# One decoder layer on one core: the program's order taken from a simulated timeline of all engines

## The chip, the core and the metric

The kernel runs on one core of a Trainium2 chip. A core has five engines with an instruction queue each: PE (matrix multiply), DVE (vector), ACT (scalar), POOL (GpSimd) and SP (here it only issues DMAs). An engine takes its own queue strictly in order and waits for the others by semaphores. The metric is the device time of one execution in microseconds (us), as the median of several.

## What is computed

One layer of a hybrid decoder, 1024 positions by 1024 channels, float32. Cut to what matters:

```python
x1 = LN1(a * x + 0.5 * swiglu(x, ffn1))             # FF = 2816, a = 2 ** 0.25
z  = x1 @ w_in                                      # 1024 x (2048 + 1824) columns
ret = silu(g) * group_norm(retention(q, k, v))      # 8 heads of 64, chunks of 128
rw  = (group_norm(rwkv7_scan(r, w, k, v, kk, a)) + bonus) * gate   # 8 heads of 64
x2 = LN2(a * x1 + concat(ret, rw) @ w_out)
x3 = LN3(a * x2 + 0.5 * swiglu(x2, ffn2))
out = x3 + sigmoid(x3 @ ple_w_gate + b) * (p @ ple_w_proj)

def step(state, inp):                               # rwkv7_scan, one position
    r_t, w_t, k_t, v_t, kk_t, b_t = inp
    sa = einsum('bhvk,bhk->bhv', state, kk_t)
    state = state * w_t - sa * b_t + v_t * k_t     # outer products
    return state, einsum('bhvk,bhk->bhv', state, r_t)
```

Each RWKV head carries a 64 by 64 state through all positions, so its chunks of 128 positions form a chain.

## The kernel before

**Stages.** The first feed-forward layer (`ffn_up`, line 152, tiles f1m; `ffn_down`, line 415, tiles f1qa, f1qb) runs to about 683 us of the profile, LN1 and the first z tiles to 757, the mixer to 1591, the second feed-forward layer (f2m, f2qa, f2qb) to 2270, and LN3 with the gated embedding (`ple`, line 1269, tile pg) to the end. Large matmuls are done in three fp32r products of operands split in two: ACT copies the high part (line 47), DVE subtracts for the low part (line 48), PE multiplies (`mm3`, lines 61, 62, 63).

**The mixer** (`mixer`, line 1205). z is made in tiles of 128 columns by `z_tile` (line 646): two raw loads on SP (line 52, raw_win), the split (hi_win, lo_win), 48 matmuls of 128x512 into tile z, an ACT copy (zs, line 659) and a store on SP (line 660). Its pools have one buffer for the split weights and one for zs, two for the raw weights, two for z. The first tiles, zf, come from `z_first` (line 662) during LN1. The gate's sums (gps, line 782) and the LoRA parts follow.

RWKV runs as eight **units** s_h, 0_0 to 3_1: a pair of heads, and one half of the 1024 positions, four chunks of 128. For a unit there are

- `rw_inputs` (line 906): smoothing, decay (ACT tanh wthw, a DVE scan csw, POOL ccw, ACT exp ePw and eMw), normalised keys (sqw, sspw, rnpw, kkw), wkw, rkw, the bonus bnpw;
- `rw_operands` (line 986): m1pw (line 1001) masked into M1 (line 1004), which is stored to device memory (line 1006, scrw), as the operands are (lines 1010 to 1016, opsw);
- `substitution` (line 1018), for two units at once: loads iltw (line 1027), 31 pairs of DVE rows (itw, line 1035, and ixw, line 1037), a store (line 1039, scsw);
- `doublings` (line 1043): loads Xd (line 1049) and M1w, then i1w to i5w on PE with DVE between (lines 1062 to 1083);
- `rw_chunks` (line 1087): for each chunk a load opsw (line 1097, four buffers), scpw on PE, masked into scz (lines 1116, 1117), then a chain through chw: lines 1122, 1125, ACT rhsw (1127), 1130, ACT saw (1132), 1134 and 1135, the next state wst (line 1144), and the outputs 1147 to 1152; at the end a group norm (`group_norm`, line 790, tile gnyw), transposes ytpw, ACT and POOL (wow, lines 1161 to 1163), and a store into mixed (line 1164).

`retention` (line 815) runs beside it. `w_out_group` (line 1182) reads rows of mixed (line 1178), splits them, and multiplies them with w_out into tile wopo, 384 matmuls in all, which DVE adds into xacc (line 1201); the last groups need mixed of units 3_0 and 3_1.

**What sets the order.** The code is written stage by stage, and a scheduler in the framework makes the order of each queue from it: of the instructions that are ready it takes the one of highest priority, where priority falls with place in the code, and advances a model of the machine. z tiles and w_out rows of a stage are **fillers**: they get a priority lower by 300 than their place would give, so they stand where nothing else is ready. The stage loop, shortened:

```python
for s in range(-1, 8):
    ...
    W[s + 2] = inputs(s + 2); self.rw_operands(W[s + 2])
    self.doublings(W[s])
    if s % 2 and s + 2 < 8: self.substitution([W[s + 1], W[s + 2]])
    self.rw_chunks(W[s], mixed[4 + u])
    with self.tc.high_priority(offset=20): self.retention(u, h, rt(u), mixed[u])
    with self.tc.issue_after(self.gate):
        for f in fill.get(s, ()):
            with self.tc.high_priority(offset=FILLER): (rw if f[0] == "w" else rt)(int(f[1]))
        ...
            with self.tc.high_priority(offset=FILLER): self.w_out_group(ks, mixed, halves, ks == (7, 3))
```

## Time and profile before

| what | us |
|---|---|
| median of 3 runs | 2381.23 (2372.49 to 2385.13) |
| the profiled execution | 2393.63 |
| its span | 2391.8 |
| PE, weight loads on PE | 2274.9 busy (95%), 1823.5 (76%) |
| DVE | 1558.6 (65%) |
| ACT | 849.5 (36%) |
| POOL | 636.0 (27%) |

Busy time is summed over the span; a matmul's end is modelled, so records of matmuls overlap. The mean granted clock of TensorE is 0.965 of full speed over the span. The slices and stretches below say where in the span an engine works, the timeline in which order, and the waits who held whom.

### The profile page before, as it was taken

To read this page: it belongs to the slowest core of one execution; us is meant where nothing else is said; L and a number is where in the kernel's file an instruction comes from. 1 tells how busy PE (TensorE), PEld (TensorE's weight loads), DVE (VectorE), ACT (ScalarE), POOL (GpSimd) and SP (SyncE) were. 2 spreads that over 40 slices of the span, in tenths; PEclk is the share of its full clock that TensorE was granted. 3 is DMA by queue.
4 is the path that set the end of the run, shared out by engine and by line. 5 is a ranking of instruction groups with operands and counts; after the bars stand their busy time and mean duration, and the time that the engine had idled before them with its cause. 6 is when DMAs were issued, how large, how long until landed. Compare 5 with 4: busy or idle time off the path is not lost.

```text
span 2391.8 us, 30775 instructions
## 1 busy us (share of the span) xinstructions
PE 2274.9 (95%) x10753; PEld 1823.5 (76%) x10753; DVE 1558.6 (65%) x2524; ACT 849.5 (36%) x1434; POOL 636.0 (27%) x535
## 2 busy tenths in 40 slices
PE   6999999999999789899899899988999999999999
PEld 5888888788786567777777677766888788788777
DVE  7677776665872365764664645779767677866962
ACT  4323323244643323232233222254322232445550
POOL 3346454100111112221222212015555543000210
PEclk8999999999999889999999887999999999999999
DMA  4355555587245545454454445232555553975321
GB/s 142 118 163 178 170 182 167 176 323 228 81 152 163 180 134 170 155 161 137 155 155 140 151 140 172 93 110 73 161 177 167 181 160 130 342 271 158 113 75 40
DMA packets 319985, 379.53 MB, mean 159 GB/s; under 512 B 36915, under 2 KB 188054, under 8 KB 319830
## 3 DMA queue, kind: packets, MB, share of 16 engines
q1 hardware_dynamic: 302576, 358.64, 46.5%
q0 software_dynamic: 3328, 12.06, 1.3%
q10 hardware_dynamic: 13926, 6.87, 1.0%
q8 instruction: 85, 1.39, 0.2%
q14 instruction: 70, 0.57, 0.1%
HBM read 256.37 MB, written 121.11 MB: 158 GB/s over the span
## 4 chain that ended last, share of the span: by engine, by line
PE 80%; DVE 11%; DMA 3%; issue 3%; ACT 2%; POOL 1%; SPq 0%; ACTq 0%; DVEq 0%; POOLq 0%
PE f1m L61 6%; PE f1m L62 6%; PE f1m L63 6%; PE f2m L61 5%; PE f2m L63 5%; PE f2m L62 5%; PE z L63 3%; PE z L61 3%; PE z L62 3%; PE f1qa L62 1%; PE f1qa L61 1%; PE f1qa L63 1%; PE scpw L1108 1%; PE pg L62 1%; PE pg L61 1%
## 5 line engine op out<-in xcount | busy, mean ns | idle before, releaser
L61 PE MATMUL z<-x1Th,hi_win 128*128 128x512 f32 x448 | 189.1, 422 | 6.9 <-ACT hi_win L47 6.9
L63 PE MATMUL z<-x1Th,lo_win 128*128 128x512 f32 x448 | 188.8, 422 | 4.9 <-DVE lo_win L48 4.9
L62 PE MATMUL z<-x1Tl,hi_win 128*128 128x512 f32 x448 | 186.7, 417 | 0.0
L61 PEld LDWEIGHTS z<-x1Th,hi_win 128*128 128x128 f32 x448 | 86.9, 194 | 28.1 <-ACT hi_win L47 8.1
L63 PEld LDWEIGHTS z<-x1Th,lo_win 128*128 128x128 f32 x448 | 86.6, 193 | 27.8 <-DVE lo_win L48 7.4
L62 PEld LDWEIGHTS z<-x1Tl,hi_win 128*128 128x128 f32 x448 | 86.8, 194 | 18.4 <-issue 1.5
L149 POOL TENSOR_TENSOR f2tb<-f2tb,f2tb 128x512 f32<-128x512 f32 x44 | 69.8, 1586 | 85.9 <-DMA f2tb<-in_ffn_w_down 77.1
L48 DVE TENSOR_TENSOR f1hl<-f1s,f1hh 128x512 fp32r<-128x512 f32 x63 | 45.5, 723 | 61.7 <-ACT f1hh L47 61.7
L48 DVE TENSOR_TENSOR lo_win<-raw_win,hi_win 128x512 fp32r<-128x512 f32 x56 | 39.9, 718 | 66.1 <-ACT hi_win L47 58.1
L149 POOL TENSOR_TENSOR f1tb<-f1tb,f1tb 128x512 f32<-128x512 f32 x44 | 70.5, 1603 | 31.7 <-DMA f1tb<-in_ffn_w_down 23.4
L48 DVE TENSOR_TENSOR f2hl<-f2s,f2hh 128x512 fp32r<-128x512 f32 x63 | 44.8, 711 | 44.6 <-ACT f2hh L47 44.6
L47 ACT CAST f1hh<-f1s 128x512 fp32r<-128x512 f32 x63 | 39.2, 622 | 91.4 <-PE f1qa L62 38.6
L47 ACT CAST f2hh<-f2s 128x512 fp32r<-128x512 f32 x63 | 39.2, 623 | 87.8 <-PE f2qa L62 35.1
L659 ACT COPY zs<-z 128x512 f32<-128x512 f32 x56 | 32.6, 583 | 103.3 <-PE z L63 84.7
L62 PE MATMUL f2qa<-f2vl,f2hh 128*128 128x512 f32 x164 | 64.1, 391 | 0.8 <-DVE f2vl L48 0.8
L63 PE MATMUL f2qa<-f2vh,f2hl 128*128 128x512 f32 x164 | 64.0, 390 | 0.6 <-DVE f2hl L48 0.6
L1143 POOL TENSOR_SCALAR sfw<-wst,few 64x64 f32<-64x64 f32 x48 | 24.0, 500 | 150.7 <-DVE wst L1144 100.1
L179 DVE TENSOR_TENSOR f1U<-f1m,f1U 128x512 f32<-128x512 f32 x50 | 33.5, 687 | 46.8 <-PE f1m L63 46.8
L62 PE MATMUL f1qa<-f1vl,f1hh 128*128 128x512 f32 x164 | 63.9, 389 | 0.0
L63 PE MATMUL f1qa<-f1vh,f1hl 128*128 128x512 f32 x164 | 63.8, 389 | 0.0
L61 PE MATMUL f1qa<-f1vh,f1hh 128*128 128x512 f32 x164 | 63.3, 389 | 0.0
L108 DVE TENSOR_TENSOR f2S<-f2w 128x512 f32<-128x512 f32 x22 | 17.7, 810 | 68.8 <-DMA f2w<-in_ffn_w_gu 64.2
(783 smaller groups left out, 7151.9 us busy)
## 6 DMA issues: line engine op xcount, KB each, us to landing
f1w<-in_ffn_w_gu SPq DMA_DIRECT2D x44, 512.0 KB
f2w<-in_ffn_w_gu SPq DMA_DIRECT2D x44, 512.0 KB
f1s<-hd SPq DMA_DIRECT2D x63, 256.0 KB
f2s<-hd SPq DMA_DIRECT2D x63, 256.0 KB
zs<-zs SPq DMA_DIRECT2D x56, 256.0 KB
opsw<-opsw SPq DMA_DIRECT2D x32, 448.0 KB
raw_win<-in_w_in SPq DMA_DIRECT2D x54, 256.0 KB
f1tb<-in_ffn_w_down SPq DMA_DIRECT2D x44, 256.0 KB
```

The source lines that it names most:

```text
L47: self.last_split = self.nc.scalar.copy(hi, src).ins
L48: (eng or self.nc.vector).tensor_tensor(out=lo, in0=src, in1=hi, op=ALU.subtract)
L61: mm(ps, a[0], b[0], start=first, stop=False)
L62: mm(ps, a[0], b[1], start=False, stop=False)
L63: mm(ps, a[1], b[0], start=False, stop=last)
L108: sub = lambda o, a, b, op=ALU.subtract: V.tensor_tensor(out=o, in0=a, in1=b, op=op)
L149: nc.gpsimd.tensor_tensor(out=t, in0=a, in1=b, op=ALU.subtract)
L179: add = lambda out, a, b, eng=V: eng.tensor_tensor(out=out, in0=a, in1=b, op=ALU.add)
L659: nc.scalar.copy(zs, ps)
L1108: nc.tensor.matmul(ps[e][:, 0:2 * P], kp[rr], ar[rr].rearrange("p a t -> p (a t)"), start=True, stop=True)
L1143: nc.gpsimd.tensor_scalar(out=sf[rr], in0=st[rr, rr], scalar1=fe[rr, c:c + 1], scalar2=None, op0=ALU.mult)
```

## The change

One argument of the context in which the program is built. With it, the scheduler advances another machine model when it picks the next ready instruction: a simulated timeline of all engines, in place of its default model. No instruction's operands change; on ACT there are two more loads of a function table (34, before 32), and the scheduler's semaphore instructions differ by some.

```diff
-    with tile.TileContext(nc) as tc:
+    with tile.TileContext(nc, schedule_with_timeline_sim=True) as tc:
         hybrid_layer(tc, A)
```

What this does to the queues is seen at three places. First, PE in the chunks of unit 0_0, chunk 3 before and chunk 2 after (chw is the chunk's chain, z the filler). Before:

```order
3609 L63 MATMUL z_0_7201<-x1Th,lo_win_1_7198 128x512
3610 L61 MATMUL z_0_7201<-x1Th,hi_win_1_7197 128x512
3611 L1130 MATMUL chw_03_7638<-rhsw_03_7642,XTw_0_7463 128x64 x2
3612 L62 MATMUL z_0_7201<-x1Tl_3704,hi_win_1_7197 128x512
3613 L63 MATMUL z_0_7201<-x1Th,lo_win_1_7198 128x512
3614 L61 MATMUL z_0_7201<-x1Th,hi_win_1_7197 128x512
3615 L1134 MATMUL chw_03_7638<-opsw_03_7626 128x128
3616 L1135 MATMUL chw_03_7638<-saw_03_7646,opsw_03_7626 128x128
3617 L62 MATMUL z_0_7201<-x1Tl_3705,hi_win_1_7197 128x512
3618 L63 MATMUL z_0_7201<-x1Th,lo_win_1_7198 128x512
```

After:

```order
3802 L61 MATMUL z_1_7975<-x1Th,hi_win_0_7937 128x512
3803 L62 MATMUL z_1_7975<-x1Tl_3700,hi_win_0_7937 128x512
3804 L1134 MATMUL chw_02_7602<-opsw_02_7590 128x128
3805 L1135 MATMUL chw_02_7602<-saw_02_7610,opsw_02_7590 128x128
3806 L63 MATMUL z_0_7947<-x1Th,lo_win_1_7944 128x512
3807 L61 MATMUL z_0_7947<-x1Th,hi_win_1_7943 128x512
3808 L62 MATMUL z_0_7947<-x1Tl_3703,hi_win_1_7943 128x512
3809 L63 MATMUL z_0_7947<-x1Th,lo_win_1_7944 128x512
3810 L61 MATMUL z_0_7947<-x1Th,hi_win_1_7943 128x512
3811 L62 MATMUL z_0_7947<-x1Tl_3704,hi_win_1_7943 128x512
```

Before, two to four z stand between two steps of the chain; after, the run that begins at 3806 has 22 z to the next chw, at 3828, and the one that ends at 3803 is as dense.

Second, DVE at the substitution for units 1_0 and 1_1 (itw and ixw are its rows, M the matrix M1, scz the chunk's masked scores, wst its state, gnyw the group norm of unit 0_1). Before:

```order
930 L802 TENSOR_REDUCE gstw_1_8444<-gsqw_1_8449 128x8
931 L804 RECIPROCAL gstw_1_8444<-gstw_1_8444 128x8
932 L805 TENSOR_TENSOR gnyw_1_8445<-gnyw_1_8445,gstw_1_8444 128x512
933 L1035 TENSOR_TENSOR itw_00_8210<-iltw_0_8198,ixw_0_8207 64x31
934 L1037 TENSOR_TENSOR ixw_0_8207<-ixw_0_8207,itw_00_8210 64x31
935 L1035 TENSOR_TENSOR itw_01_8213<-iltw_0_8198,ixw_0_8207 64x60
936 L1037 TENSOR_TENSOR ixw_0_8207<-ixw_0_8207,itw_01_8213 64x30x2
937 L1035 TENSOR_TENSOR itw_02_8216<-iltw_0_8198,ixw_0_8207 64x87
```

After:

```order
909 L1004 COPY_PREDICATED M_6343<-mask,m1pw_10_8089 128x512
910 L1004 COPY_PREDICATED M_6343<-mask,m1pw_11_8090 128x512
911 L1144 SCALAR_TENSOR_TENSOR wst_6360<-chw_10_8320,few_1_6794,sfw_100_8332 64x64
912 L1144 SCALAR_TENSOR_TENSOR wst_6360<-chw_10_8320,few_1_6794,sfw_101_8335 64x64
913 L754 SCALAR_TENSOR_TENSOR wvw_0_8870<-wzvw_0_8867,pcol,smvw_0_8871 128x512
914 L1116 COPY_PREDICATED scz_6347<-mask,scpw_120_8382 128x256
915 L1035 TENSOR_TENSOR itw_00_8210<-iltw_0_8198,ixw_0_8207 64x31
916 L1037 TENSOR_TENSOR ixw_0_8207<-ixw_0_8207,itw_00_8210 64x31
917 L1117 COPY_PREDICATED scz_6347<-mask,scpw_120_8382 128x128
918 L1116 COPY_PREDICATED scz_6349<-mask,scpw_121_8383 128x256
```

Before, the substitution begins behind unit 0_1's group norm, 22 rows behind M1 (910); after, five rows behind M1, among the masks of unit 0_1's third chunk, and the group norm stands behind it, at 1004 to 1010.

Third, PE at the end of the last unit (ytpw and ytpr are the transposes of the last RWKV and retention outputs, wopo the w_out matmuls). Before:

```order
5323 L812 MATMUL ytpw_1_12573<-ident,gnyw_1_12563 128x128 x4
5324 L855 MATMUL rspr_11_12633<-zqr_1_12595,zkr_1_12605 128x128
5325 L855 MATMUL rspr_10_12632<-zqr_1_12595,zkr_1_12605 128x128
5326 L855 MATMUL rspr_11_12633<-zqr_1_12595,zkr_1_12605 128x128
5327 L855 MATMUL rspr_10_12632<-zqr_1_12595,zkr_1_12605 128x128
5328 L855 MATMUL rspr_11_12633<-zqr_1_12595,zkr_1_12605 128x128
5329 L61 MATMUL wopo_1_0_0_11795<-mw 128x512
5330 L62 MATMUL wopo_1_0_0_11795<-mw 128x512
```

After:

```order
5539 L1152 MATMUL chw_13_12546<-saw_13_12554,scz_6351 128x64
5540 L1151 MATMUL chw_13_12546<-opsw_13_12534,scz_6353 128x64
5541 L1152 MATMUL chw_13_12546<-saw_13_12554,scz_6353 128x64
5542 L812 MATMUL ytpw_1_12573<-ident,gnyw_1_12563 128x128 x4
5543 L812 MATMUL ytpr_1_12685<-ident,gnyr_1_12670 128x128 x4
5544 L61 MATMUL wopo_1_0_0_12982<-mw 128x512
5545 L62 MATMUL wopo_1_0_0_12982<-mw 128x512
5546 L61 MATMUL wopo_1_1_0_12990<-mw 128x512
```

Before, 336 of the 384 wopo matmuls stand behind ytpw; after, 48 do, from 5544 to 5591, and the others stand among units 2_1, 3_0 and 3_1.

## Rows read from the trace of the kernel before

**Rows 1.** The page's slices: tenths of each fortieth of the span (59.8 us) that PE was busy.

```profile
PE   6999999999999789899899899988999999999999
```

**Rows 2.** Stretches, PE. Columns: stretch, length, PE busy (matmul records), granted clock, DMA share, GB/s.

```profile
100.00:460.00 360.00, 360.00 (x1590) 1.00 0.50 163
...
757.00:872.00 115.00, 92.83 (x354) 0.87 0.54 172
872.00:922.00 50.00, 49.23 (x313) 0.93 0.49 152
922.00:1038.00 116.00, 108.70 (x592) 0.96 0.48 150
...
1398.00:1447.00 49.00, 47.30 (x276) 0.79 0.51 152
1447.00:1502.00 55.00, 54.98 (x285) 0.75 0.43 140
...
872.00:1502.00 630.00, 597.72 (x3381) 0.92 0.48 149
...
1057.00:1085.00 28.00, 27.89 (x177) 1.00 0.49 144
```

**Rows 3.** The same view for the z tiles' matmuls alone.

```profile
872.00:1502.00 630.00, 287.20 (x975) 0.92 0.48 149
...
1057.00:1085.00 28.00, 11.81 (x41) 1.00 0.49 144
```

**Rows 4.** The same view for the w_out matmuls (wopo) alone, behind the last unit.

```profile
1502.00:1592.00 90.00, 83.35 (x337) 1.00 0.32 106
```

**Rows 5.** PE in order of time: start, duration, engine, line, tiles; z matmuls, first i1.

```profile
1014.48 0.39 PE L61 MATMUL z<-x1Th,hi_win 128*128 128x512 f32 x1
...
1018.68 0.39 PE L61 MATMUL z<-x1Th,hi_win 128*128 128x512 f32 x1
...
1037.97 1.95 PE L1062 MATMUL i1w<-Xd,M1w 128*128 128x128 f32 x16
```

**Rows 6.** Stretches, PE's weight loads: stretch, length, PEld busy (records), granted clock.

```profile
100.00:460.00 360.00, 298.01 (x1589) 1.00 0.50 163
872.00:1502.00 630.00, 466.55 (x3380) 0.92 0.48 149
```

**Rows 7.** In order of time, all engines, behind the last unit: transposes to store.

```profile
1502.31 0.60 PE L812 MATMUL ytpw<-ident,gnyw 128*128 128x128 f32 x4
...
1507.63 0.32 SPq L1164 DMA_DIRECT2D mixed<-wow  x1
```

**Rows 8.** The same for the inputs of unit 2_0, first and last step.

```profile
1036.81 0.67 ACT L935 ACTIVATE wthw<-wpw,pder 128x512 f32<-128x512 f32 x1
...
1055.97 1.49 PE L1001 MATMUL m1pw<-arw,bbw 64*128 64x128 f32 x16
```

**Rows 9.** The same for two steps of a chunk of unit 0_1.

```profile
983.51 0.27 ACT L1127 COPY rhsw<-chw 128x128 f32<-128x128 f32 x1 [0.46 <-PE chw L1125]
...
983.83 0.66 PE L1130 MATMUL chw<-rhsw,XTw 128*128 128x64 f32 x4
```

**Rows 10.** The same on PE at LN1's second half: two of four groups.

```profile
686.98 0.60 PE L80 MATMUL tp<-ident,f1acc 128*128 128x128 f32 x4
...
689.75 0.60 PE L80 MATMUL tp<-ident,f1acc 128*128 128x128 f32 x4
```

**Rows 11.** The same, the substitution run in unit 0_1: M1's store, first row, its store.

```profile
968.77 0.34 SPq L1006 DMA_DIRECT2D scrw<-M  x1
...
990.78 0.18 DVE L1035 TENSOR_TENSOR itw<-iltw,ixw 64x31 f32<-64x31 f32 x1
...
1029.21 0.47 SPq L1039 DMA_DIRECT2D scsw<-ixw  x1
```

**Rows 12.** Waits, 757 to 1591: who waited for whom, us, times, longest.

```profile
SPq L660 <- ACT zs L659: 139.7, 33, 13.0
...
DVE wst L1144 <- PE chw L1135: 36.7, 15, 6.1
```

## The prediction

> **What bounds the kernel now.** I read the 40 slices first [rows 1]. PE's digit is 9 at both sides of the middle of the span; slices 12 to 27, the mixer, are the only long stretch with lower ones. The change is one line, but it gives every engine's queue a new order. Comparing the two orders, PE's is the same or nearly so in both feed-forward layers; rows move by hundreds of places only in the mixer, by some tens where LN1, the second feed-forward layer and the last stage begin. So the question is what the mixer, 757 to 1591 us, gives up.
>
> The mixer is eight RWKV units in a chain. I take a unit from its first i1 matmul to the next unit's: 50, 116, 47, 132, 53, 128, 49, 55 us 630 in all (the stretches of the first two, the last two and all eight stand in [rows 2]). The even ones are short; the odd ones are long, because the substitution for the next two units runs in them on DVE, and PE has little left but z matmuls. Then come 89 us of w_out matmuls, from 1502 to 1591 [rows 4, 7].
>
> How idle is PE in those 630 us? The busy column says 597.7 of 630 [rows 2], so 32 idle. I don't believe that as the amount to gain: a z matmul is listed as 0.39 us, but 18 of them start within 4.20, 0.23 apart [rows 5], so the ends overlap, and before a wait the modelled end covers a part of it. I therefore count by starts. A z or a w_out matmul, of one shape, costs 0.23. The small fp32 matmuls are two records each; 16 records of i1 take 1.95 [rows 5], 16 of m1p 1.49 [rows 8], and 136 of them share 28 us of unit 1_0 with 41 z, which leaves them 18.6 or 0.136 each, short waits included [rows 2, 3]. I take 0.12, ends 0.10 and 0.136. In the units stand 3381 records, 975 of z, 48 of w_out, so 2358 small ones [rows 2, 3]: 224 + 11 + 283 = 518 us of work, and 112 of idle (ends 74 and 159).
>
> The Trainium skill ("Perfetto Trace Analysis", Identifying the Most-Contended Engine) says that matmul busy time is no good measure because matmuls are pipelined, and to go by the share of weight loads. That share is 83% where PE never waits (298 of 360, from 100 to 460) and 74% in the units (467 of 630) [rows 2, 6]: by that, 11% or about 67 us idle. If the three kinds of idle below shrink in the same proportion, 72 becomes 43, the small work 328, and the units end 16 us later: 2344. The trace agrees that the busy column misleads; on the amount the two readings differ.
>
> **The change part by part.** Work is the same on all engines but two table loads more on ACT. What moves:
>
> 1. *The fillers.* Counted in the two orders between the first i1 of each unit, z (with the first tiles' zf): ahead of unit 0_0 514 before and 566 after; in the units 974 and 922. The w_out matmuls: in the units 48 before and 336 after; behind the last recurrence row 336 and 48. So 288 of 384 w_out matmuls leave the tail, 288 x 0.23 = 66 us, and go between the steps of units 2_1, 3_0 and 3_1, from which 52 z make room.
>
> 2. *The tail.* Now 1502 to 1591 holds 337 w_out matmuls [rows 4], 78 us of work and 11 of everything else. After: 48 matmuls, 11 us. But the last rows of mixed come only behind the last group norm, and that chain loses its cover: from the last ytp at 1502.3 by ACT, two POOL rows and other POOL work between to the store at 1507.6 [rows 7], 4 without that; a store, the load behind it and the first use take 8.8 elsewhere (1029.2 to 1038.0) [rows 5, 11]. So with the split 14 us are exposed. LN2 and the first transposes, which now lie beside w_out matmuls, may be late by 5. 11 + 14 + 5 = 30 instead of 89: **-59** (ends -72 with the chain covered by the last retention rows, -45 if chain and LN2 take 14 more).
>
> 3. *The units.* Filler work after: (922 + 336) x 0.23 = 289, before 235; small work unchanged, 283. Idle after, in three pieces. (a) In six units the new order has a part with almost no fillers: doublings, the next unit's inputs and the first chunk, some 75 small matmuls, before the fillers start. The inputs chain is tanh to m1p, 1036.8 to 1057.5 in unit 1_0, step by step through ACT, DVE and POOL [rows 8], so this part is about 22 us with 138 records x 0.12 = 16.6 of work: 5.4 idle x 6 = 32. (b) In the filled part each gap between chunk steps holds 13 to 23 z, 3 to 5 us, where the trace shows 0.5 to be needed: rhs on ACT 983.51 to 983.78 behind one chw, the next chw at 983.83 [rows 9]. There PE should be the bound. I take 5%, the share that is idle even by the busy column (32 of 630) [rows 2], of 390 us: 20. (c) Units 3_0 and 3_1 now have 104 us, 76 fillers and 485 small records [rows 2], so 29 idle; 74 more fillers take about 9 of it: 20. Sum 72 us idle, and units of 289 + 283 + 72 = 644: **+14**. No waits in (b) and half of (a): -22; 10% in (b): +34.
>
> 4. *Ahead of unit 0_0.* 52 more z is +12 us of work. 757 to 872 has 92.8 us busy of 115 even by the busy column [rows 2], so there is room; the new order puts 118 more z in the first wait behind the gate sums and 52 more between the second m1p and i1, where 130 stand now. I take -15. Against that, at LN1's second half four groups of transposes come 2.75 us apart, filled with 10 zf each [rows 10]; after, most zf run earlier and 12 are left: +7. Together **-8** (ends -20, +10).
>
> 5. *The substitution.* Before, it starts behind the group norm: M1 is stored at 968.8, and the loads follow, but the first DVE row comes at 990.8 and the store behind the last at 1029.2, then Xd and i1 at 1038 [rows 5, 11]. After, its rows start some five DVE rows behind M1 and lie among the chunk's masks and states. The chain of an odd unit is then inputs 22, M1 to loads 8, its own rows with others between as now 38, to i1 9: 77 us. The unit's PE work, about 85, is longer, so it is hidden and costs nothing more. It is what lets the odd units fall from 116 to 132 to some 80 to 90; the even ones grow to as much.
>
> 6. *Start of both feed-forward layers, LN3 and the last stage.* Places move by up to 76 there, and the tables on ACT are two loads more. PE in the start of the second layer has its own waits; I take 0, ends -8 and +8.
>
> Sum: -59 + 14 - 8 = **-53**. On the profiled execution, 2393.6, that gives 2341; the median of the runs is 12 lower, so 2381.2 - 53 = **2328 us**.
>
> **Rivals.** *A, the fillers cover more:* no waits in the filled parts, a better clock: units -22, front -20, tail -65: -107, 2274. For it: the granted clock is 0.75 and 0.79 in the last two units, which have fewest fillers, and 0.96 from 922 to 1038 with many z [rows 2]; a unit with more fillers may be granted more. Against: the parts with no fillers remain.
>
> *B, the new order idles as large a share as the old:* 112 of 630, 17.8%. Then the units take 572 / 0.822 = 696, +66, and nothing is left of the tail: 2381 - 59 + 66 - 8 = 2380. For it: the 72 are a count on an order, and the order fixes who is ahead of whom on SP too. SP stood 13.0 us behind one z store, 139.7 in 33 such waits [rows 12], with the loads of operands and weights queued behind. In the new order each z store still waits for its filler, and PE reaches fillers later relative to the chunk.
>
> *C, slower: the substitution in DVE's queue.* Its 62 rows now stand among masks and states that wait for PE; states alone wait 36.7 us, 15 times, for chunk matmuls [rows 12], and these now stand behind 3 to 5 us of fillers. If 14 more such waits of 4 us fall between the first and the last row, the chain grows from 77 to 133 and the unit from 85 to 133, and with three substitutions that is +144: 2472. It decides from 26 us a substitution on: 8 until the chain is longer than PE's work, then 53 / 3 = 18; at 33 the time is 2402. Against it: in unit 0_1 the order has few such rows ahead of the first half of the substitution.
>
> *D, nothing changes:* excluded by the order, unless the moves cancel.
>
> **How the numbers follow.** Forecast, 2290 to 2362: 0.48. A, 2250 to 2290: 0.17. B, 2362 to 2393: 0.2. C: 0.15, mostly 2393 to 2450. The range leaves out a fifth, the lowest part of A and most of C: 2262 to 2400. A measurement of this kernel tells about 0.5%, 12 us, from no change. Faster than 2369: 0.48 + 0.17 + 0.09 = 0.74; within: 0.11; slower: 0.15.
>
> **What would show it.** Right: the last ytp row to the first f2tp row about 30 us instead of 89; eight units near 644 us, the odd ones under 95; PE's idle by starts down by about 40 there; i1 of unit 0_0 near 864. Step 3 is wrong if PE waits inside the filled parts (chw on DVE or ACT), B shows as SP waits on zs with opsw or raw_win late, C as itw rows spread over more than 60 us and PE waiting for Xd. The tail is wrong if w_out waits for mw by more than 10.

## The result, and the profile after

The changed kernel takes 2466.47 us (median of 4 runs, 2454.08 to 2470.07); the kernel before, on the same chip, 2377.55. The ratio is 1.0362 with a 95% interval of 1.0314 to 1.041: slower by 3.6%, where 2328 was forecast and a range to 2400. The profiled execution has a span of 2465.2 us; before it was 2391.8, so there the difference is 73.4. The medians lie 88.9 apart: the profiled execution of the kernel before, 2393.63 us, is 16 above its median, so the stretches below understate the loss by about that.

The page of the changed kernel: each engine's busy time, share of the span and instructions; then, in slices of 61.6 us, PE's busy tenths and the granted clock of TensorE in tenths of full speed.

```profile
PE 2306.3 (94%) x10753; PEld 1872.9 (76%) x10753; DVE 1547.6 (63%) x2524; ACT 841.6 (34%) x1432; POOL 644.3 (26%) x535
...
PE   6999999999989799899899899868999999999899
...
PEclk8999999999989899798699899769999999999999
```

The clock's line of the kernel before:

```profile
PEclk8999999999999889999999887999999999999999
```

PE is as busy as ever by the busy column, and the digits of [rows 1] are hardly changed. What is new stands in the clock's line: in slices 15 to 27, the mixer's units, it has two 7s and two 6s, where the line of before has one 7 there. The busy column can't tell whether a matmul ran at 2.4 GHz or at 1.2.

Stretches of the kernel after, PE (stretch, length, PE busy and records, granted clock, DMA share, GB/s): the first feed-forward layer, the eight units, the two parts of unit 1_1, units 3_0 and 3_1, and the tail. They answer to [rows 2].

```profile
100.00:460.00 360.00, 349.85 (x1530) 0.99 0.52 161
...
902.70:1628.30 725.60, 670.96 (x3659) 0.88 0.44 133
...
1188.60:1228.30 39.70, 37.30 (x170) 0.59 0.43 131
1228.30:1284.40 56.10, 56.10 (x301) 0.95 0.46 136
1494.30:1562.20 67.90, 59.75 (x351) 0.87 0.23 71
1562.20:1628.30 66.10, 54.40 (x312) 0.76 0.15 48
1628.30:1655.20 26.90, 15.99 (x56) 0.66 0.67 216
```

The same for the z matmuls alone, then for the w_out matmuls alone, in the units:

```profile
902.70:1628.30 725.60, 242.69 (x923) 0.88 0.44 133
```

```profile
902.70:1628.30 725.60, 91.67 (x336) 0.88 0.44 133
```

Against the profile of before this gives four differences, which add up to the 73.4:

| stretch | before, us | after, us | difference | forecast |
|---|---|---|---|---|
| start to the first i1 of unit 0_0 | 872.1 | 902.7 | +30.6 | -8 |
| eight units | 630.2 | 725.6 | +95.4 | +14 |
| tail, last ytpw to the first f2tp | 89.0 | 26.9 | -62.1 | -59 |
| second feed-forward layer to the end | 800.5 | 810.0 | +9.5 | 0 |

So the tail is given back as forecast, and the units lose one and a half times as much. Much of that is work which the tail gave up; what the change costs on the whole stands under "One account for all". Where in a unit? Its first part, from the first i1 to the last m1p, has no z at all in unit 1_1 (170 records, none a z), and its clock is 0.59. PE there in 6 us stretches, same columns:

```profile
1188.00:1194.00 6.00, 6.00 (x22) 0.50 0.19 67
1194.00:1200.00 6.00, 4.95 (x32) 0.84 0.67 218
1200.00:1206.00 6.00, 5.01 (x46) 0.73 0.54 149
1206.00:1212.00 6.00, 6.00 (x21) 0.50 0.09 38
1212.00:1218.00 6.00, 5.64 (x20) 0.50 0.47 152
1218.00:1224.00 6.00, 6.00 (x22) 0.50 0.66 202
1224.00:1230.00 6.00, 6.00 (x25) 0.50 0.30 76
```

and some of the instructions in them, in order of time (start, duration, engine, line, tiles):

```profile
1187.65 1.12 PE L812 MATMUL ytpw<-ident,gnyw 128*128 128x128 f32 x4 [5.14 <-DVE gnyw L805]
...
1214.98 1.11 PE L1130 MATMUL chw<-rhsw,XTw 128*128 128x64 f32 x4
1216.45 0.80 PE L1134 MATMUL chw<-opsw 128*128 128x128 f32 x2 [0.35 <-ACT saw L1132]
...
1221.20 2.07 PE L1001 MATMUL m1pw<-arw,bbw 64*128 64x128 f32 x8
...
1226.81 2.07 PE L1001 MATMUL m1pw<-arw,bbw 64*128 64x128 f32 x8
1228.81 0.79 PE L61 MATMUL z<-x1Th,hi_win 128*128 128x512 f32 x1
```

Ahead of the part PE waits 5.14 us for the group norm, and the clock falls there, from 1.00 (1176 to 1182) to 0.50. It rises once more and falls again, and from 1206 on PE has an instruction under way nearly all the time: the longest wait from there to 1230 is 0.35 us. But four chw matmuls take 1.11 us, 0.66 in [rows 9], and a run of eight m1p takes 2.07, where such a run takes 1.16 in this kernel at full clock (at 919.3 and at 924.5): 1.7 and 1.8 times as long. The sixteen m1p, 4.14 us here, take 1.49 in [rows 8] also because they stand in one run there; the order alone makes them 2.32. In [rows 2] unit 1_0 has a stretch with 41 z among 136 such records, and its clock is 1.00.

### The profile page after: what moved, and what is told of

It reads as the page before. It is cut to its first block, busy times and chain, and to the rows that moved or that the text cites. A ratio compares the mean times of both kernels' runs of the same rounds, so it can differ in the third digit from the quotient of the medians.

```text
span 2465.2 us, 30772 instructions
## 1 busy us (share of the span) xinstructions
PE 2306.3 (94%) x10753; PEld 1872.9 (76%) x10753; DVE 1547.6 (63%) x2524; ACT 841.6 (34%) x1432; POOL 644.3 (26%) x535
## 4 chain that ended last, share of the span: by engine, by line
PE 75%; DVE 10%; DMA 6%; issue 3%; ACT 2%; POOL 2%; SPq 1%; DVEq 0%; POOLq 0%; ACTq 0%
PE f1m L61 4%; PE f1m L62 4%; PE f1m L63 4%; PE z L61 4%; PE z L62 4%; PE z L63 4%; PE f2m L61 4%; PE f2m L62 4%; PE f2m L63 4%; PE scpw L1108 2%; PE f2qa L61 2%; PE f2qa L62 2%; PE f2qa L63 2%; PE f1qa L63 2%; PE f1qa L62 2%
## 5 line engine op out<-in xcount | busy, mean ns | idle before, releaser
L63 PE MATMUL z<-x1Th,lo_win 128*128 128x512 f32 x448 | 180.7, 406 | 0.5 <-DVE lo_win L48 0.4
L149 POOL TENSOR_TENSOR f2tb<-f2tb,f2tb 128x512 f32<-128x512 f32 x44 | 66.2, 1504 | 104.6 <-DMA f2tb<-in_ffn_w_down 95.2
L149 POOL TENSOR_TENSOR f1tb<-f1tb,f1tb 128x512 f32<-128x512 f32 x44 | 65.5, 1489 | 101.0 <-DMA f1tb<-in_ffn_w_down 92.6
L108 DVE TENSOR_TENSOR f2S<-f2w 128x512 f32<-128x512 f32 x22 | 17.4, 793 | 111.2 <-DMA f2w<-in_ffn_w_gu 81.6
L108 DVE TENSOR_TENSOR f1S<-f1w 128x512 f32<-128x512 f32 x22 | 18.2, 831 | 101.2 <-DMA f1w<-in_ffn_w_gu 51.6
L61 PE MATMUL wopo<-mw 128*128 128x512 f32 x128 | 56.6, 442 | 16.1 <-ACT mw L47 9.7
L1201 DVE SCALAR_TENSOR_TENSOR xacc<-wopo,xacc 128x512 f32<-128x512 f32 x64 | 43.5, 683 | 31.8 <-PE wopo L63 31.7
```

The costliest lines, as they stand in the source:

```text
L61: mm(ps, a[0], b[0], start=first, stop=False)
L63: mm(ps, a[1], b[0], start=False, stop=last)
L108: sub = lambda o, a, b, op=ALU.subtract: V.tensor_tensor(out=o, in0=a, in1=b, op=op)
L149: nc.gpsimd.tensor_tensor(out=t, in0=a, in1=b, op=ALU.subtract)
L1201: nc.vector.scalar_tensor_tensor(out=a, in0=po, scalar=1.0 / ALPHA, in1=a, op0=ALU.mult, op1=ALU.add)
```

## The experiments

Each is a small edit of the kernel after or of the kernel before; the ratio is against runs of the kernel before on the same chip (2377 to 2386 us). The kernel after was timed on one chip, so where a time is compared with its 2466, a few us can be the chip's. A profile is one execution: that of the fillers at -100, that of the fillers from i1 and that of the last experiment below took 22, 16 and 25 us more than the median of their runs.

**Which stretch loses it.** The kernel before, with only the first up layer under the simulated timeline:

```diff
+        with tc.block(name='upf', schedule_with_timeline_sim=True):
-        up("f1", A["ffn1_w_gu"][0], A["ffn1_w_down"][0], load1, None, lambda h: xc[h].close())
+            up("f1", A["ffn1_w_gu"][0], A["ffn1_w_down"][0], load1, None, lambda h: xc[h].close())
```

> The kernel before, with its first up layer (to 462 us) in a block of its own, ordered by the simulated timeline, the rest by the default model as before. The order in the block is that of the changed kernel. Theory A (the 17 us that the changed kernel lost there come from the order of this layer alone): PE's waits for f1U come up, the last f1m matmul is 15 to 19 us later than before, the whole +15 to +35 us with what the boundary of the block costs. Theory B (the loss is due to what comes later in the queues): no waits there, the whole only longer by the boundary, under 12.

2390.89 us, ratio 1.0049 (1.0028 to 1.0069), 9.5 us for the 15 to 35 of theory A. In its profile the first i1 of unit 0_0 starts at 889.5, 17.4 later than before, and PE has the stop that the kernel after has (waits, 100 to 470: who waited for whom, us, times, longest):

```profile
PE f1m L61 <- DVE f1U L179: 8.6, 2, 4.7
```

Next, the first down layer, LN1 and the mixer in one block, the rest in the default order; once with the timeline, once with the default model (False in that line of the diff), to tell the cost of having a block from that of the timeline:

```diff
+        with tc.block(name="part", schedule_with_timeline_sim=True):
             xs = [ExitStack() for _ in range(3)]
...
             xacc = L.mixer(x1T, zs, mixed, x1, lambda pool: normalise2(0, pool))
```

> The kernel before, with all between the first up layer and the second (down layer, LN1, mixer) in a block ordered by the simulated timeline; both up layers and the end by the default model. To be read against the same block with the default model (e10). From the changed kernel's trace: LN1 +6, to the first i1 +6, units +95, tail -62: e9 is 35 to 55 us above e10. If the loss of the units hangs on delays brought from the first layer or on the whole program's order, within 15 us.

> The same block as in e9, ordered by the default model: what the two boundaries cost. Counts of z and w_out in the units are those of before to within 10. Expected 5 to 25 us above before, with units and tail within 6 us of before.

2446.18 us, 1.028 (1.0245 to 1.0315), with the timeline; 2377.33, 0.9988 (0.9963 to 1.0013), without. So the block costs nothing, where 5 to 25 us were expected, and 69 us come from the timeline in this part (35 to 55 expected) and 9.5 from the up layer; together 78 of 89. The units under the timeline, and both stretches of the default block (units, tail):

```profile
887.80:1619.00 731.20, 684.96 (x3663) 0.86 0.43 133
```

```profile
872.90:1487.70 614.80, 584.03 (x3381) 0.94 0.49 153
1487.70:1576.90 89.20, 85.61 (x388) 1.00 0.33 106
```

731.2 against 614.8 us, and a tail of 26.4 against 89.2: this block alone repeats what the whole change does there. The default block has the same numbers of records as the kernel before in its units, which took 630.2 there: so much can two profiles differ.

**What a filler costs in a unit.** The kernel after, with the w_out rows of the last three units held back until the last chunk matmul of unit 3_1:

```diff
-                    for ks, halves in rows.get(s, ()):
+            with self.tc.issue_after(self.lastch):
+                for s in (5, 6, 7):
+                    for ks, halves in rows[s]:
```

> The changed kernel, with the w_out matmuls put back behind the recurrence: they may start behind the last chunk matmul of unit 3_1, so that 360 of 384 stand behind the last recurrence row (336 before the change, 48 after it). Units 2_1, 3_0 and 3_1 lose 312 w_out matmuls. Theory A (a filler costs its full time in a unit, since PE waits for the chain or runs it and has no idle that a filler could use): the tail grows by 72 us, the three units shrink by about 72, the whole stays within 10 us of the changed kernel. Theory B (that of the prediction: fillers stand in idle time): the units shrink by 30 to 40 only, the whole grows by 30 to 40.

2486.54, 1.0425 (1.0392 to 1.0458): 20 us slower than the kernel after, between theory A (within 10) and theory B (30 to 40). Units and tail:

```profile
902.40:1577.60 675.20, 604.24 (x3347) 0.85 0.45 138
1577.60:1668.50 90.90, 86.02 (x369) 1.00 0.34 109
```

312 w_out fewer in the units save 50.4 us there (725.6 to 675.2) and add 64.0 to the tail. At 0.23 they are 72 us of work, so most of a filler's time is paid in the units too. The other direction, the kernel before with 108 w_out moved from the tail into the units by another priority of the fillers (which also moves 74 z from the units to ahead of unit 0_0):

```diff
-FILLER = -300
+FILLER = -100
```

> The kernel before (default model) with the fillers' priority lowered by 100 instead of 300: 588 z ahead of unit 0_0 instead of 514, 228 w_out matmuls behind the last recurrence row instead of 336. If a shorter tail is worth its matmuls, 108 x 0.23 = 25 us, less what the units take for 108 more w_out (25 us, less their idle): -10 to -20 us. If the units give it all back, within 6 us of before. The first parts of the units hold fewer z than before (0, 38, 8, 29, 7, 26 instead of 28, 52, 15, 120, 7, 121), so theory 1 expects a lower clock in 1_1 and 2_1, some 5 us each.

2382.09, 1.0004 (0.9973 to 1.0036): the tail falls from 89.0 to 64.2, the units grow to 652.0, the first i1 comes 17.8 later, and by the medians nothing is gained. The share of the tail in the change, -62, is therefore for the most part not a gain of itself.

**Is it the clock of the first parts?** The kernel after, with the fillers of a unit released by its first i1 and not by its last m1p:

```diff
-                nc.tensor.matmul(ps[:, i * P:(i + 1) * P], M1[:, 4 * q + i], self.Xd[:, 4 * q + i], start=True, stop=True)
+                ins = nc.tensor.matmul(ps[:, i * P:(i + 1) * P], M1[:, 4 * q + i], self.Xd[:, 4 * q + i], start=True, stop=True)
+                if q == i == 0:
+                    self.gate = ins.ins
```

> The changed kernel, but the fillers of a stage may start behind the first i1 matmul of its unit instead of behind its last m1p matmul. Of the order only this changes: the first parts (i1 to m1p) of units 0_1, 1_0, 1_1 and 2_0 get 91 z matmuls each instead of 0, 13, 0 and 43, and the second parts lose as many; all ahead of unit 0_0 stays. Theory 1 (granted clock): the first parts are long because PE runs small matmuls at half clock there, and so does the start of the second part; with z matmuls in them the clock stays near 1.0, units 0_1, 1_0, 1_1 go from 94 to 97 us to about 82 each and 2_0 loses a few us; the whole -30 to -45 us against the changed kernel. Theory 2 (waits of the in-order queues of DVE and SP): the first part grows by the 21 us of z, the second part loses them, the units stay within 4 us each and the whole within 10.

2463.52, 1.0344 (1.0294 to 1.0394): 3 us less than after, where theory 1 wanted 30 to 45; the total is that of theory 2. The first parts now hold 91 z and stand at a clock of 0.95, as meant, but units 0_1 to 2_0 fall only from 386.7 to 373.6 in the profile. Now something else is late (PE waits, units):

```profile
PE ytpw L812 <- DVE gnyw L805: 50.9, 8, 8.2
PE vtpr L812 <- DMA zvr<-zs: 15.1, 1, 15.1
```

The fillers are spent in the first part, and at the end of the unit PE stands for the group norm, 27.5 us in 5 waits in the kernel after. In unit 0_1 DVE's queue has the transpose for the next unit in the middle of the group norm, and that waits for the substitution's matrix from memory (DVE, then PE). Wait and transpose are about 2.8 of PE's 8.25 us; the rest is the group norm's own rows:

```profile
1096.19 1.25 DVE L1053 STREAM_TRANSPOSE XTw<-Xd 128x1024 f32<-128x1024 f32 x1 [1.61 <-DMA Xd<-scsw]
...
1101.18 0.69 DVE L805 TENSOR_TENSOR gnyr<-gnyr,gstr 128x512 f32<-128x512 f32 x1
```

```profile
1101.09 1.11 PE L812 MATMUL ytpw<-ident,gnyw 128*128 128x128 f32 x4 [8.25 <-DVE gnyw L805]
```

To give PE work there without taking it from elsewhere, 48 needless matmuls of the z shape were added behind the first i1 of units 0_0 to 2_0, 240 in all or 55 us:

```diff
+                    if s < 5:
+                        with self.tc.issue_after(self.first), self.tc.high_priority(offset=FILLER):
+                            ps = self.ptile("z", f"warm{s}", 2)
+                            for i in range(48):
+                                self.nc.tensor.matmul(ps, x1T[1][i % KT][:, 0:P], x1T[0][i % KT][:, 0:HALF], start=i == 0, stop=i == 47)
```

> The changed kernel with 48 matmuls of 128x512 more in the first part of units 0_0 to 2_0 (operands that are there, a result that nobody reads: 240 matmuls, 55 us of PE work that the layer doesn't need). Theory 1 (granted clock): the clock stays near 1.0 in the first parts; i1 to the last m1p of units 0_1, 1_0, 1_1 takes 26 to 28 us instead of 31, 30 and 38, though 11 us of work are added; the whole between -20 and +10 us. Theory 2 (queues, or the latency of the inputs' chain): the first parts stay at 30 to 38 or grow, and the whole grows by 20 to 45 us.

2494.1 us, 1.0463 (two runs), 28 more than after: on the whole theory 2's range. All units and the first parts of 1_0 and 1_1 (in the kernel after 31.8 us at a clock of 0.75, and 39.7 at 0.59):

```profile
903.90:1652.80 748.90, 702.07 (x3900) 0.92 0.42 129
1112.10:1143.40 31.30, 31.30 (x191) 1.00 0.52 157
1207.80:1248.20 40.40, 39.46 (x198) 0.80 0.38 115
```

In 1_0, 11 us of added work cost nothing: the part takes 31.3 us at full clock with it and took 31.8 at 0.75 without. In 1_1 they cost 0.7 at a clock of 0.80. In 0_1 they cost 8: 40.7 us at 0.79, 32.6 at 0.66 without. Over all units 55 us of work cost 23. So added work that raises the clock pays for much of itself, the most direct sign here that the low clock is a cause and no mere companion; that it doesn't pay for all of the added work is plain too, and theory 1's 26 to 28 us a part were not reached.

**Fillers kept for the unit's end.** The kernel after, with the last z tile of each stage held behind the unit's last chunk matmul:

```diff
+                    with self.tc.issue_after(self.gate if n < cut else self.lastch), self.tc.high_priority(offset=FILLER):
+                        z(c)
```

> The changed kernel with the last z tile of each stage (48 matmuls) held back behind the last chunk matmul of its unit; the z counts of the units change by 4 to 12 only, but some 12 to 40 z now stand at a unit's end, where PE waited for the group norm, and in the first part of the next. Theory A (what is lost in the units is PE's wait for the group norm, 27.5 us in five units, and the low granted clock in the first parts, some 45 us): both fall by half or more, the whole -15 to -35 us. Theory B (the chain through DVE and the substitution sets the units' length, and the fillers' place doesn't matter): within 8 us of the changed kernel.

2456.64, 1.0296 (1.0272 to 1.032), 10 us less than after and between the ranges of the two theories. The waits for the group norm fall to 11.4 us, and the units 0_0 to 2_0 from 482.5 to 464.2, while 2_1 to 3_1 take back 16 of these 18. The clock of the units is no better, 0.87.

**The first up layer.** The subtractions of the second operands (L149, on POOL) and their loads and stores (L147, L150, in SP's queue) stand closer to the weights' splits than before. First the stores alone, then loads and stores on POOL's queue instead of SP's:

```diff
-            nc.sync.dma_start(wt[i, f], t)
+            nc.gpsimd.dma_start(wt[i, f], t)
```

> The changed kernel with the stores of the recombined down weights (line 150) issued by POOL, which computes them, instead of by SP. Theory: in the first up layer SP stands behind such stores with the next load of up weights queued behind (DVE waits 11 us twice, PE stops for f1U); with the stores off SP the f1m waits go, the up layer ends 15 us earlier, the whole -15 to -22 us. Rival: the stop comes from POOL's own bursts of these subtractions; then PE's waits stay and the whole stays within 6 us, or POOL's issues make it longer.

> The changed kernel with loads and stores of the down weights' recombination (lines 147 and 150) issued by POOL, so that SP holds nothing ahead of the loads of up weights but the hidden values' stores. Theory A (SP's queue order delays the up weights, DVE starves, PE stops): PE has no waits for f1U or f1G between 100 and 460 us, the first up layer ends about 15 us earlier, the second 5, the whole -15 to -22 us. Theory B (POOL's own bursts delay its splits): the waits stay, the whole within 6 us, or longer by POOL's 176 issues.

2467.95, 1.0348 (1.0308 to 1.0387), and 2473.84, 1.0363 (1.0328 to 1.0398): no change by either, and PE's waits in the layer stay, 7.9 and 9.9 us. Their place in SP's queue is not the cause. Then the kernel after without the 44 subtractions of the first layer (this part of the computation is left out):

```diff
-            nc.gpsimd.tensor_tensor(out=t, in0=a, in1=b, op=ALU.subtract)
+            if nm != "f1":
+                nc.gpsimd.tensor_tensor(out=t, in0=a, in1=b, op=ALU.subtract)
```

> The changed kernel without POOL's 44 subtractions of down weights in the first layer (line 149; the blocks are stored as loaded, so the first down layer multiplies with other weights, in the same time). Theory A (these subtractions stand ahead of POOL's splits of up weights, and so PE waits): the waits for f1U go, the last f1m is 12 to 17 us earlier than in the changed kernel, the whole -10 to -18 us. Theory B (the up weights' loads come late because SP's queue and the four raw buffers give them no lead): waits and time stay within 5 us.

2446.91, 1.0273 (1.0244 to 1.0302), 20 us less than after. PE is busy for all of 100 to 460 at full clock, as in [rows 2]:

```profile
100.00:460.00 360.00, 360.00 (x1590) 1.00 0.52 167
```

and the last f1qa matmul starts at 694.6 (682.5 before, 711.5 after). In the kernel after, POOL has this between 207 and 217 us, and DVE stands until a store of such a tile has read it:

```profile
207.67 4.03 POOL L149 TENSOR_TENSOR f1tb<-f1tb,f1tb 128x512 f32<-128x512 f32 x3 [0.93 <-DMA f1tb<-in_ffn_w_down]
211.65 1.30 POOL L48 TENSOR_TENSOR f1A12l<-f1w,f1A12h 128x512 fp32r<-128x512 f32 x1
```

```profile
215.32 0.69 DVE L108 TENSOR_TENSOR f1S<-f1w 128x512 f32<-128x512 f32 x1 [10.97 <-DMA wt<-f1tb]
```

So the subtractions are the cause in this layer; whether by their place in POOL's queue or by the stores behind them that DVE waits for, this run doesn't separate.

**The default order with other first parts.** Last, the kernel before, where the first i1 of a unit may only come behind the last z of the stage before:

```diff
+                            self.lastfill = self.lastmm
...
-                    self.doublings(W[s])
+                    with self.tc.issue_after(self.lastfill):
+                        self.doublings(W[s])
```

> The kernel before, its default order kept, but the first i1 matmul of a unit may only come behind the last z matmul of the stage before. This was meant to leave the first parts of the units without fillers; the new order shows something else: the inputs of later units move ahead by one, and every unit from 0_0 to 2_0 has some 100 z between its first i1 and its last m1p, and 40 to 90 behind it (before: 28, 52, 15, 120 and 7 ahead of the last m1p). Fillers: ahead of unit 0_0 624 (514 before), in the units 864 z and 111 w_out (974 and 48), in the tail 273 w_out (336). So it is a third way to spread the same fillers, with no part of units 0_0 to 2_0 unfilled. Theory 1 (a filler costs its 0.23 us of PE wherever it stands; beside that only the half granted clock of unfilled parts costs): ahead of unit 0_0 +5 to +25 for 110 more z, in the units -11 for 47 fewer fillers and -5 to -15 for the clock (49.6 us lost to it in the profile of before, mostly in units 3_0 and 3_1, which stay thin), tail -14: 2355 to 2385. Rival (an order with filled first parts is held by the chain i1, doublings, chunks, group norm, substitution, as the odd units were where i1 opened the fillers in the changed kernel): units of 0_1 to 2_0 about 90 to 95 each, the same sum as before for four of them, but 2_1 to 3_1, with 12 fillers or so in each chunk's place, at half clock: +20 to +45: 2400 to 2425.

2462.16, 1.0309 (1.0264 to 1.0355): as slow as the change, in the default model, with fewer fillers in the units. Both theories missed it by 37 or more. In the profile the first i1 comes 44 us later than before, where 5 to 25 were expected, and the units take 71 more. The units, and the first part of 0_1 in stretches of 8 us:

```profile
916.50:1617.50 701.00, 638.37 (x3281) 0.82 0.42 128
```

```profile
1018.00:1026.00 8.00, 8.00 (x31) 0.50 0.10 37
1026.00:1034.00 8.00, 8.00 (x24) 0.50 0.18 56
1034.00:1042.00 8.00, 8.00 (x30) 0.50 0.30 90
```

That part has 102 z, but 7 of them stand in these 24 us and most of the rest behind: a count of fillers by part, on which I had based my expectation, says little. How they are spread may say more; no run here varies that alone.

No kernel here is faster than the kernel before; two are equal to it.

**One account for all.** For the units of eleven profiles: fillers (z, w_out and needless) at 0.23 us and the other records at 0.12, as in the prediction, are the work at full clock; (1 - granted clock) x length is what the clock took (to 4 us or so, since the clock is given to two digits); the rest is what remains.

| kernel | units, us | fillers | other records | work | clock | taken by the clock | rest |
|---|---|---|---|---|---|---|---|
| before | 630.2 | 1023 | 2358 | 518 | 0.92 | 50 | 62 |
| before, up layer by timeline | 617.9 | 1023 | 2358 | 518 | 0.93 | 43 | 56 |
| before, block, default | 614.8 | 1023 | 2358 | 518 | 0.94 | 37 | 60 |
| before, fillers at -100 | 652.0 | 1056 | 2329 | 522 | 0.91 | 59 | 71 |
| before, i1 behind the last z | 701.0 | 976 | 2305 | 501 | 0.82 | 126 | 74 |
| after | 725.6 | 1259 | 2400 | 578 | 0.88 | 87 | 61 |
| block by timeline | 731.2 | 1262 | 2401 | 578 | 0.86 | 102 | 50 |
| after, fillers from i1 | 728.8 | 1259 | 2400 | 578 | 0.90 | 73 | 78 |
| after, needless matmuls | 748.9 | 1499 | 2401 | 633 | 0.92 | 60 | 56 |
| after, w_out held back | 675.2 | 947 | 2400 | 506 | 0.85 | 101 | 68 |
| after, last z held back | 723.4 | 1259 | 2401 | 578 | 0.87 | 94 | 52 |

The rest stays between 50 and 78 while the units go from 615 to 749. What moves them is the work placed in them and the clock. This is a sum, and stretches at the low clock hold waits as well as work, so it does not prove each column's cause; the needless matmuls and the held-back w_out are the interventions behind it.

Most of the 60 us of work that the change adds to the units come out of the tail; on the whole program the work is the same, 10753 matmul records in either profile. Every run has its span and its mean granted clock on record, so the same sum can be made over the whole span (us):

| kernel | runs | taken by the clock | mean | span less that | mean |
|---|---|---|---|---|---|
| before | 46 | 59 to 98 | 74 | 2301 to 2315 | 2308 |
| after | 4 | 132 to 153 | 145 | 2315 to 2320 | 2318 |
| block, default | 10 | 71 to 91 | 77 | 2298 to 2306 | 2301 |
| block by timeline | 4 | 141 to 157 | 147 | 2297 to 2299 | 2298 |
| after, fillers from i1 | 4 | 118 to 136 | 126 | 2335 to 2341 | 2338 |
| after, needless matmuls | 2 | 115 to 125 | 120 | 2369 to 2376 | 2373 |
| after, last z held back | 4 | 140 to 153 | 146 | 2309 to 2312 | 2311 |

Of the 81 us between the first two means, 71 are the clock's; of the mixer's block by timeline all are. The 240 needless matmuls add their 55 us of work, and 25 come back by the clock. So what the change costs goes nearly all with the low clock, and even the runs of the one kernel before differ mostly by it. In this sum, too, a wait at the low clock counts half as the clock's, and it doesn't tell why the new order is granted less.

## Why the prediction was wrong

*What bounds the kernel.* Right that the mixer decides, and that the busy column shows too little idle. But the idle that I counted by starts, 112 us, was taken for waits that fillers could cover. By the account above 50 of it was the clock, a term that the sum of step 3 doesn't have.

*Step 1, the fillers.* Right: 923 z and 336 w_out in the units, 48 in the tail.

*Step 2, the tail.* Right in size and chain: 26.9 us for a forecast 30. From ytpw to the store of mixed (all engines, in order of time), 5.0 us for 5.3 in [rows 7]:

```profile
1628.32 1.12 PE L812 MATMUL ytpw<-ident,gnyw 128*128 128x128 f32 x4 [6.50 <-DVE gnyw L805]
...
1633.27 0.32 SPq L1164 DMA_DIRECT2D mixed<-wow  x1
```

*Step 3, the units.* This failed: +95 for +14. The filler work was right (+54 forecast, 236 x 0.23 = 54). The idle was to fall from 112 to 72; by the same count it rose to 148. Its three pieces were:
(a) six unfilled parts at 22 us each, priced with 0.12 us a record. That price came from a stretch at a clock of 1.00 [rows 2]. The six took 31 on average, 188 us in all, at clocks from 0.59 to 1.00; by (1 - clock) x length, 45 of the 188 are the clock's, and 143 remain for a forecast of 132. The step priced small matmuls at full clock wherever they stand. That the fillers which the order takes out of these parts had kept the clock up there fits the rows (the two parts at 1.00 hold 49 and 43 z) and the needless matmuls in unit 1_0, but is not shown for each part. Rival A held half of this thought, that more fillers bring a better clock, and drew the wrong sign from it.
(b) The six filled parts: 404 us, near the 390 with 20 of idle that I had taken: right, and PE's waits for chw on DVE and ACT come to only 7.8 us in the units.
(c) Units 3_0 and 3_1: 134 us for some 113. Their clock is 0.87 and 0.76, which takes 25.
The sum closes: 60 more of work at full clock (236 fillers and 42 other records), 37 more for the clock, 1 less of rest, 96. Over the whole program, where the work cancels, the clock is 71 of the 81 us.

*Step 4, ahead of unit 0_0.* From the last matmul of the first layer to the first i1, 191.2 us after and 189.6 before: +2 for a forecast -8. LN1's second half loses 6, for 7 forecast. Between, 35 us are behind at LN1's last transposes (701.9 before, 737.1 after), 30 of them are made up until the first gate sums (756.8 and 762.2), where fewer z stand, and 25 are paid again from there to i1 (115.3 and 140.5), where they went.

*Step 5, the substitution.* It was hidden in the changed kernel, as forecast: no wait for Xd among PE's waits in the units. With the first parts filled (first experiment on the clock), its matrix holds DVE for 1.61 us in the middle of unit 0_1's group norm, and units 0_1 to 2_0 took 85 to 97 each. Whether it would bound shorter units is not shown.

*Step 6, starts of the layers.* Wrong: the last matmul of the first layer starts 29 us later. 17.4 of it are the up layer alone, by its own run; the block with the down layer ends that layer 13 later under the timeline (696.7 for 683.4), which is about the rest, though not by what. I saw that rows move by tens there and compared only PE's order. The rows that cost in the up layer were POOL's. The table loads on ACT were read the wrong way round: the traces have 34 before and 32 after, two fewer. Behind the tail 9.5 us more are unexplained; they are at the edge of the 8 that I allowed.

*The rivals.* B came nearest in its thought, that the idle doesn't go away: it gave the units 696 us at a share of 17.8%, and they took 725.6 with a share of 148, 20%. B's sign is absent: SP waits 122.7 us on zs, 40 times, from 762 to 1655, against 139.7 in [rows 12], and PE waits in the units for neither opsw nor raw_win. C, the only one on the slower side, came near the time by another way: of its signs, PE never waits for Xd in the units, and the itw rows spread over 31, 34 and 58 us, none over 60. The weight-load share, which the Trainium skill ("Perfetto Trace Analysis", Identifying the Most-Contended Engine) recommends, is 552.1 of 725.6 or 76% in the units after, 74% before [rows 6]: it reads as a little less idle. The trace agrees in so far as the rest in the table hardly moves, 62 and 61, but the share doesn't show the time that went to the clock.

## What to carry to other kernels

Fillers taken from a tail into a chain are not free: they cost their own time there unless that chain really waits, so move some and measure before counting the tail as gained. When an order puts fillers together, look at what is left without them, and price those stretches at the clock that the trace grants to such work without fillers, not at the duration beside them. Make the sum of clock and span over the whole run first: it shows at once how much of a loss goes with the clock. And compare the orders of every engine, POOL's as well, in stretches where the bottleneck's own order is unchanged.

## What the runs showed of the hardware

TensorE's granted clock has two levels in these traces, 0.50 (1.2 GHz) and 1.00 (2.4 GHz). In unit 1_1 of the kernel after it was 1.00 from 1176 to 1182 and fell in the 5.14 us wait for the group norm: 0.81 from 1182 to 1188, where PE is busy for 0.85 us. The Trainium skill ("TensorE: Matmul & The Clock Gate", HAM oscillation — how this bites in real kernels) lays the low clock to idle gaps between bursts of matmuls; the trace agrees for this fall.

What the gaps seen here don't explain is what follows. With small fp32 matmuls alone the clock rose (0.84 from 1194 to 1200), fell again, and stayed at 0.50 for the 24 us from 1206 to 1230, while PE's records followed each other with no wait over 0.35 us. At the z matmuls behind them it came back: 0.71 from 1230 to 1236, and 0.95 over the second part of the unit. The ends of matmul records are modelled, so waits can be hidden in them; whether the clock stayed low for such waits or for the kind of work, no run here separates.
